# An encoder trunk on one core: thirteen weight units split ahead by half units, five output-weight units split where they are used, and attention's visits in another order

## The chip, the core and the metric

The kernel runs on one core of one Trainium2 chip. The metric is device time of one execution in microseconds (us). The engines are named as in the profile: PE is TensorE (PEld its weight loads), DVE is VectorE, ACT is ScalarE, POOL is GpSimd, and SP is SyncE, which issues the DMA transfers. "Granted clock" is the share of full speed at which the profile shows TensorE clocked.

## The reference

One inference step of a two-layer encoder for two groups of frames, 1024 of a prompt and 32 of a sample. Layer 0 mixes with an mLSTM, layer 1 with windowed attention (16 query heads, 2 key heads, its own chunk of 64 frames and the two before). Behind each mixer stands an output product and a LayerNorm, then a gated FFN and a LayerNorm. What the change touches of it:

```python
D_MODEL, D_FF, DEPTH = 1024, 2816, 2

def swiglu(x, w_gu, w_down):
    g, u = jnp.split(x @ w_gu, 2, axis=-1)
    return (jax.nn.silu(g) * u) @ w_down

def sink_attention(q, k, v, sinks, bias):
    s = jnp.einsum('bcqhgd,bckhd->bchgqk', q, k).astype(F32) * (HEAD_DIM ** -0.5) + bias
    sk = sinks.astype(F32).reshape(N_KV_HEADS, GROUP)[:, :, None, None]
    mx = jnp.maximum(jnp.max(s, -1, keepdims=True), sk)
    p = jnp.exp(s - mx)
    p = p / (jnp.sum(p, -1, keepdims=True) + jnp.exp(sk - mx))
    return jnp.einsum('bchgqk,bckhd->bcqhgd', p.astype(v.dtype), v)

def swa_prompt(x, k, v, w_q, sinks, w_out, slopes):
    q = (x @ w_q).reshape(B, nc, CHUNK, N_KV_HEADS, GROUP, HEAD_DIM)
    ...
    o = sink_attention(q, kw, vw, sinks, bias)
    return o.reshape(B, T, D_ATT) @ w_out

def trunk(...):
    for layer in range(DEPTH):
        ...
        x = layer_norm(DEEPNORM_ALPHA * x + mix, ln_g[layer, 0], ln_b[layer, 0])
        x = layer_norm(DEEPNORM_ALPHA * x + swiglu(x, w_gu[layer], w_down[layer]), ln_g[layer, 1], ln_b[layer, 1])
```

All of it is in fp32.

## The kernel before, in words

**Numbers.** Every fp32 operand of a dense product is split into a high part (a cast to fp32r) and a low part (the operand less its high part, also fp32r). A k step of `gemm` is then three matmuls: high by high (L433), high by low (L434), low by high (L435). So each weight and each activation needs a cast and a subtraction ahead of its use. Activations live as `act` (fp32) and `sx` (both parts), `split_act` makes the second from the first (cast L463, subtraction L464). The 1056 columns of activations go in three groups `GRP` of 384, 384 and 288 for projections, and in four quarters of 264 for output products.

**Order.** One host-side program emits all instructions; each engine runs its own in the order of emission. The dense products are emitted one behind the other, and each k step calls `tick(us)` with its written length. Other work stands in generator tasks, launched on a `Weave`: a task emits some instructions and yields the us until it wants to go on, so that written pauses, not a scheduler, set where its instructions stand among the dense ones. `drain` runs a task ahead without pauses until a condition holds.

**Weights.** A weight unit is 128 rows by 1024 columns, split as two half units (u,0) and (u,1) of 128x512. The class `Weights` loads units into a ring of four raw tiles `wr` and makes, in one fixed order, the split tiles `wh`, `wl` (L250 to L260): the cast on ScalarE (L258), or on GpSimd (L256) for halves listed in `on_gpsimd`, which is empty before; the subtraction on VectorE for halves in `on_vector` and on GpSimd else (both L260). `home` tiles (`oh`) hold the halves that stay resident. Units listed in `ready` are not split there: their parts are read from a tile in DRAM, `halves`.

**The split ahead.** `split_before` (L1312 to L1330) fills `halves` during layer 0's FFN. It is launched at the FFN's seventh factor product, stands beside the FFN's up product, and covers 18 units: 2 of `wkv`, 8 of `wqb` (query weights), 8 of `wout_b` (attention's output weights). It has one raw tile `wraw` of 128x1024 and one tile `whi` of 128x512. For a unit it loads `wraw`, yields 9.0, and for each half casts into `whi` (L1322), yields 1.5, subtracts in place (L1324), yields 1.8, stores both parts (L1327) and yields 4.5 or 2.0.

**The down product.** Behind the up product, `down` multiplies by the FFN's second weight through seven factor products of half size. Its `put` adds each PSUM tile (A or B) to `act` on VectorE: L1587 for the first sum of a cell, L1589 for the others.

**Attention.** Sixteen heads go in eight pairs, j. A visit (jp, g) is the pairs j = 2jp and 2jp+1 in column group g: `q_group` projects the queries (24 matmuls for each j), and six items of attention follow, three blocks of 128 frames for each j. An item passes six stages in a pipeline: `scores` (matmuls L1879 or L1885 into `psS`, then the bias and a row maximum on VectorE), `soft` (exponent on ScalarE), `scale` (L1910 on VectorE, L1913 or L1917 on GpSimd), `turn` (transposes L1938 into T, cast L1942, subtraction L1943), `values` (L1967 into O), `place` (L1981 on ScalarE, L1985 on VectorE, adding into `act`). `scores` and `turn` yield `GAP_A` = 0.46 us an item, `values` twice that for every second item. The visits go in the order `JG`:

```python
JG = [(jp, 0) for jp in range(4)] + [(jp, g) for jp in range(4) for g in (1, 2)]
```

**The early output tiles.** After a visit (jp, 2) with jp below `EARLY` = 3, `before(0)` sees to it that all of attention's group 0 is placed and its activations are split, and one tile of the output product's first quarter is emitted (`out_tile`, L1265). The rest of the output product, `mixer_out` (L1272), follows after the last visit, with the LayerNorm beside it. `mixed_parts` (L1232) is the task that splits attention's result: 24 casts on ScalarE and 24 subtractions on GpSimd. Unit lists: `U_QB` are query weights, `U_OUT_B[0]` the output weights for the first three quarters, `U_OUT_B[1]` the same weights a second time for the last.

## Time and profile before

| what | value |
|---|---|
| runs | 3: 2203.27, 2203.59, 2203.68 us |
| median | 2203.59 us |
| profiled execution | 2202.94 us |
| its span (first to last recorded instruction) | 2201.2 us |
| mean granted clock of TensorE | 0.995 |

The profiled execution stands beside the runs, 0.65 us below their median; all durations quoted below are of it. In its rows, "A <- B" at a tile reads "A is written from B", x is a count, and a row of the timeline is: start in us from the span's start, duration, engine, line, operation, tiles, shapes, and in brackets how long the engine had been idle just ahead and who ended that. The row of a window gives its limits and length, then busy us and instructions of PE, PEld, DVE, ACT and POOL, the granted clock, the mean share of the 16 DMA engines and GB/s.

### The profile page before, as it was taken

How to read it: one execution, taken by the hardware profiler on the slowest of the kernel's cores; microseconds unless marked ns; L12 is line 12 of the kernel's file. 1: busy time of each engine (PE TensorE's matmuls, PEld its weight loads, DVE VectorE, ACT ScalarE, POOL GpSimd, SP SyncE). 2: the span in 40 equal slices, each digit the busy share in tenths (PEclk: the TensorE clock that was granted, in tenths of full speed). 3: DMA queues.
4: the chain of work that ended last, by engine and by line, in shares of the span. 5: the costliest groups of instructions: out<-in, count | busy, mean ns of one | idle time of the engine just before them, and what ended most of it. 6: DMA issues, size and time to landing. Idle time of an engine off the chain costs nothing.

```text
span 2201.2 us, 44080 instructions
## 1 busy us (share of the span) xinstructions
PE 2166.9 (98%) x16982; PEld 2142.1 (97%) x16982; DVE 1469.2 (67%) x2822; ACT 995.0 (45%) x2243; POOL 917.1 (42%) x928
## 2 busy tenths in 40 slices
PE   9999999999999999989999999999999999999997
PEld 9999999999999999989999999999999999999997
DVE  4465676788777776556657776788666566466657
ACT  4443455465444444321235676656444444431125
POOL 2544310004666665444432443500665555554441
PEclk9999999999999999999999999999999999999999
DMA  5221212212665666797617542611344433497712
GB/s 171 77 63 57 58 40 87 89 39 86 216 220 204 226 207 208 267 329 263 190 52 234 163 126 85 223 49 39 128 147 157 147 138 147 137 350 249 251 53 80
DMA packets 191250, 332.99 MB, mean 151 GB/s; under 512 B 19200, under 2 KB 124728, under 8 KB 191040
## 3 DMA queue, kind: packets, MB, share of 16 engines
q1 hardware_dynamic: 186688, 325.84, 44.3%
q10 hardware_dynamic: 4352, 4.33, 0.6%
q8 instruction: 134, 2.20, 0.4%
q14 instruction: 76, 0.62, 0.1%
HBM read 226.47 MB, written 101.82 MB: 149 GB/s over the span
## 4 chain that ended last, share of the span: by engine, by line
PE 87%; DVE 5%; DMA 4%; ACT 3%; issue 1%; SPq 0%; POOL 0%; ACTq 0%; DVEq 0%; POOLq 0%
PE d L433 11%; PE d L435 10%; PE d L434 10%; PE A L433 9%; PE A L435 9%; PE A L434 9%; PE B L433 7%; PE B L434 7%; PE B L435 7%; PE O L1967 1%; DMA sx<-hs_t 1%; PE psS L1879 1%; PE T L1938 1%; ACT act L536 1%; PE T L986 1%
## 5 line engine op out<-in xcount | busy, mean ns | idle before, releaser
L260 POOL TENSOR_TENSOR wl_s<-wr,wh_s 128x512 fp32r<-128x512 f32 x224 | 309.9, 1394 | 250.9 <-ACT wh_s L258 194.8
L433 PE MATMUL d<-sx,wh 128*128 128x264 f32 (+2 forms) x1040 | 331.9, 319 | 0.0
L260 POOL TENSOR_TENSOR wl_a<-wr,wh_a 128x512 fp32r<-128x512 f32 x112 | 158.5, 1419 | 395.3 <-ACT wh_a L258 390.2
L435 PE MATMUL d<-sx,wl 128*128 128x264 f32 (+2 forms) x1040 | 316.5, 304 | 2.4 <-POOL wl L260 2.4
L434 PE MATMUL d<-sx,wh 128*128 128x264 f32 (+2 forms) x1040 | 316.0, 304 | 0.5 <-POOL sx L464 0.5
L433 PE MATMUL A<-sx,wh_s 128*128 128x264 f32 x896 | 255.7, 285 | 4.5 <-DVE act L1587 4.5
L434 PE MATMUL A<-sx,wh_s 128*128 128x264 f32 x896 | 255.2, 285 | 0.0
L435 PE MATMUL A<-sx,wl_s 128*128 128x264 f32 x896 | 255.0, 285 | 0.0
L258 ACT CAST wh_s<-wr 128x512 fp32r<-128x512 f32 x224 | 135.5, 617 | 193.5 <-DVE wr L201 99.2
L433 PEld LDWEIGHTS d<-sx,wh 128*128 128x128 f32 x1040 | 196.4, 189 | 3.1 <-ACT wh L258 0.2
L435 PEld LDWEIGHTS d<-sx,wl 128*128 128x128 f32 x1040 | 195.8, 188 | 3.2 <-POOL wl L260 2.9
L434 PEld LDWEIGHTS d<-sx,wh 128*128 128x128 f32 x1040 | 196.6, 189 | 1.8 <-POOL sx L464 0.7
L433 PE MATMUL d<-sx,ex 128*128 128x264 f32 x624 | 180.8, 290 | 0.1
L434 PE MATMUL d<-sx,ex 128*128 128x264 f32 x624 | 177.2, 284 | 0.0
L435 PE MATMUL d<-sx,ex 128*128 128x264 f32 x624 | 176.9, 284 | 0.0
L433 PEld LDWEIGHTS A<-sx,wh_s 128*128 128x128 f32 x896 | 169.6, 189 | 4.7 <-ACT wh_s L258 4.7
L435 PEld LDWEIGHTS A<-sx,wl_s 128*128 128x128 f32 x896 | 169.8, 190 | 0.0
L434 PEld LDWEIGHTS A<-sx,wh_s 128*128 128x128 f32 x896 | 169.6, 189 | 0.0
L1383 POOL TENSOR_TENSOR z<-z 128x528 fp32r<-128x528 f32 x76 | 104.8, 1380 | 116.7 <-ACT z L1382 101.4
L433 PE MATMUL A<-ex,wh_s 128*128 128x264 f32 x448 | 127.5, 285 | 0.0
L434 PE MATMUL A<-ex,wh_s 128*128 128x264 f32 x448 | 127.1, 284 | 0.0
L435 PE MATMUL A<-ex,wl_s 128*128 128x264 f32 x448 | 127.1, 284 | 0.0
(374 smaller groups left out, 7155.4 us busy)
## 6 DMA issues: line engine op xcount, KB each, us to landing
wr<-in_gu SPq DMA_DIRECT2D x92, 512.0 KB, 4.0
hs_x<-z SPq DMA_DIRECT2D x72, 528.0 KB, 3.0
hs_t<-z SPq DMA_DIRECT2D x64, 528.0 KB, 3.2
sx<-hs_x SPq DMA_DIRECT2D x112, 264.0 KB, 5.8
sx<-hs_t SPq DMA_DIRECT2D x64, 264.0 KB, 6.2
ex<-hs_t SPq DMA_DIRECT2D x64, 264.0 KB, 6.1
wr<-in_dn SPq DMA_DIRECT2D x32, 512.0 KB, 6.1
wh<-halves SPq DMA_DIRECT2D x46, 256.0 KB, 2.9
```

What stands on the lines that cost most here:

```text
L258: self.nc.scalar.copy(hi, r)
L260: eng.tensor_sub(lo, r, hi.bitcast(F32))
L433: nc.tensor.matmul(out, ah, bh, start=start and k == 0, stop=False, **kw)
L434: nc.tensor.matmul(out, ah, bl, start=False, stop=False, **kw)
L435: nc.tensor.matmul(out, al, bh, start=False, stop=stop and k == last, **kw)
L536: nc.scalar.activation(z, z, AF.Identity, scale=gk, bias=bk)
L986: nc.tensor.matmul(pc[:, : 2 * (DV + 1)], keys, vt[j][:, c], start=True, stop=True)
L1383: eng.tensor_sub(lo.bitcast(F32R), buf(s), hi)
L1879: nc.tensor.matmul(ps[:rows, at : at + nk], lhs, k[:, k0 : k0 + nk], start=i == 0, stop=i == 1)
L1938: nc.tensor.transpose(pt[:nk, t, :rows], p[:rows, at : at + nk], ident[:rows, :rows])
L1967: nc.tensor.matmul(out, v[:nk], x, start=i == 0, stop=i == len(todo) - 1)
```

## The change

1. *Split ahead.* It covers 13 units (of `wout_b` only the first three), and goes by half units with two raw tiles of 128x512, each next half being loaded two us of written time ahead of the cast of the one at hand. There is still one `whi`. `stored` counts halves.
2. *Late output weights.* The other five `wout_b` units of `U_OUT_B[0]` are loaded raw and split in `_next`: half 0 with its cast on ScalarE and its subtraction on VectorE, half 1 with both on GpSimd. The halves of the first two units of `U_OUT_B[1]` have their subtractions on VectorE in place of GpSimd.
3. *Activation splits of attention's result.* Of 24 subtractions the even k go to VectorE, the odd k stay on GpSimd. Casts of group 0 with even k go to GpSimd.
4. *Visits.* The first four stay, then (0,2), (0,1), (1,2), (1,1), (2,2), (2,1), (3,1), (3,2). An early output tile follows the visits (1,2), (2,2) and (3,2) in place of (0,2), (1,2) and (2,2). The gap is 0.43 us, and 0.45 from the seventh visit on.

```diff
--- before.py
+++ after.py
@@ -46,7 +46,7 @@
 RAW = 4
 SLOTS = 5
 GAP_M = (0.6, 1.666, 1.519, 1.5)
-GAP_A = 0.46
+GAP_A = (0.43, 0.45)
 
 FEED_W = 1.7
 
@@ -232,7 +232,7 @@
         ready = u in self.ready
         self.load_to(u if f in (0, 1) else u + 1)
         if ready:
-            assert self.ready[u] in self.stored
+            assert (self.ready[u], f) in self.stored
             w = self.units[u].shape[-1] // 2
         else:
             r = self._source(u, f)
@@ -371,18 +371,20 @@
         U_QB[0] += [add("wqb", u) for u in range(b, b + 4)]
     for jp in range(QH // 4):
         U_QB[1] += [add("wqb", 2 * jp + i) for i in range(2)]
-        if jp < EARLY:
-            U_OUT_B[0].append(add("wout_b", jp))
+        if 0 < jp <= EARLY:
+            U_OUT_B[0].append(add("wout_b", jp - 1))
     U_OUT_B[0] += [add("wout_b", u) for u in range(EARLY, 8)]
     U_OUT_B[1] += [add("wout_b", u) for u in range(8)]
     add_ffn(1)
     on_vector.update((u, f) for u in U_O + U_OUT_A[0] for f in range(2))
     on_vector.update((u, f) for u in U_OUT_B[1][2:] for f in range(2))
     on_vector.update((u, f) for u in U_Q[:1] for f in range(2))
-    W = Weights(nc, base, units, pairs, on_vector, set())
-    BEFORE = [("wkv", i) for i in range(2)] + [("wqb", i) for i in range(8)] + [("wout_b", i) for i in range(8)]
-    for us in (*U_KV, *U_QB, U_OUT_B[0]):
-        name = "wkv" if len(us) == 2 else "wqb" if us is not U_OUT_B[0] else "wout_b"
+    on_vector.update((u, f) for u in U_OUT_B[1][:2] for f in range(2))
+    on_vector.update((u, 0) for u in U_OUT_B[0][EARLY:])
+    W = Weights(nc, base, units, pairs, on_vector, {(u, 1) for u in U_OUT_B[0][EARLY:]})
+    BEFORE = [("wkv", i) for i in range(2)] + [("wqb", i) for i in range(8)] + [("wout_b", i) for i in range(EARLY)]
+    for us in (*U_KV, *U_QB, U_OUT_B[0][:EARLY]):
+        name = {2: "wkv", 8: "wqb", EARLY: "wout_b"}[len(us)]
         W.ready.update((u, BEFORE.index((name, i))) for i, u in enumerate(us))
     W.early = {up[i] for up in U_UP for i in range(FIRST, FT)}
     wv.feed = W.feed
@@ -459,8 +461,8 @@
         gemm(ps, wcols(u), xcols(g))
         return ps
 
-    def split_act(k, g, low=nc.vector):
-        nc.scalar.copy(sxh[k][g][:], act[k][g][:])
+    def split_act(k, g, low=nc.vector, high=nc.scalar.copy):
+        high(sxh[k][g][:], act[k][g][:])
         low.tensor_sub(sxl[k][g][:], act[k][g][:], sxh[k][g][:].bitcast(F32))
 
 
@@ -1229,7 +1231,7 @@
 
     WHOLE = [(g, range(KT)) for g in range(3)]
 
-    def mixed_parts(src, free, mixed, pauses, low=(nc.vector,), runs=WHOLE):
+    def mixed_parts(src, free, mixed, pauses, high=(nc.scalar.copy,), low=(nc.vector,), runs=WHOLE):
 
 
         for (g, ks), pause in zip(runs, pauses):
@@ -1239,7 +1241,7 @@
             for k in ks:
                 while not mixed(k, g):
                     yield 0.3
-                split_act(k, g, low[k % len(low)])
+                split_act(k, g, low[k % len(low)], nc.scalar.copy if g else high[k % len(high)])
                 if g == 0:
                     nc.sync.dma_start(act[k][g], src[:, k, t0 : t0 + n])
                 elif k % 4 == 3:
@@ -1313,20 +1315,31 @@
 
         ex = ExitStack()
         p = ex.enter_context(pool("before"))
-        raw, hi = new(p, "wraw", [P, D]), new(p, "whi", [P, D // 2], F32R)
-        for i, (name, idx) in enumerate(BEFORE):
-            nc.sync.dma_start(raw[:], A[name][idx])
-            yield 9.0
-            for f in range(2):
-                r = raw[:, f * (D // 2) : (f + 1) * (D // 2)]
-                nc.scalar.copy(hi[:], r)
-                yield 1.5
-                nc.vector.tensor_sub(r.bitcast(F32R), r, hi[:].bitcast(F32))
-                yield 1.8
-                for k, t in enumerate((hi[:].bitcast(F32), r)):
-                    nc.sync.dma_start(W.halves[:, i, f, k, :], t)
-                yield 2.0 if f else 4.5
-            W.stored.add(i)
+        raws = [new(p, f"wraw{i}", [P, D // 2]) for i in range(2)]
+        hi = new(p, "whi", [P, D // 2], F32R)
+        todo = [(i, f) for i in range(len(BEFORE)) for f in range(2)]
+
+        def load(n):
+            i, f = todo[n]
+            name, idx = BEFORE[i]
+            nc.sync.dma_start(raws[n % 2][:], A[name][idx][:, f * (D // 2) : (f + 1) * (D // 2)])
+
+        load(0)
+        yield 4.0
+        for n, (i, f) in enumerate(todo):
+            yield 3.0
+            if n + 1 < len(todo):
+                load(n + 1)
+            yield 2.0
+            r = raws[n % 2][:]
+            nc.scalar.copy(hi[:], r)
+            yield 1.5
+            nc.vector.tensor_sub(r.bitcast(F32R), r, hi[:].bitcast(F32))
+            yield 1.8
+            for k, t in enumerate((hi[:].bitcast(F32), r)):
+                nc.sync.dma_start(W.halves[:, i, f, k, :], t)
+            W.stored.add((i, f))
+            yield 3.7
         ex.close()
 
     def ffn(layer, li, tasks, lx, final):
@@ -1841,13 +1854,19 @@
 
     ast = {"ready": 0, "scored": 0, "placed": 0, "v": 0, "visit": -1}
 
-    JG = [(jp, 0) for jp in range(4)] + [(jp, g) for jp in range(4) for g in (1, 2)]
+    JG = [(jp, 0) for jp in range(4)] + [(jp, g) for jp in range(4) for g in ((2, 1) if jp < 3 else (1, 2))]
     QG = [(2 * jp + i, g) for jp, g in JG for i in range(2)]
 
     def last_item(j, g):
         return 6 * JG.index((j // 2, g)) + 6
 
-    def attention(gap):
+    gaps = [[0.0] * 8, [0.0] * 8]
+
+    def pace(gap):
+        gaps[0][:] = [gap] * 8
+        gaps[1][:] = [0.0, 2 * gap] * 4
+
+    def attention():
         S, pairs_ = {}, {}
 
         def parts(b):
@@ -1989,11 +2008,11 @@
         yield from pipeline(
             [(2 * jp + i, 3 * g + b) for jp, g in JG for b in range(3) for i in range(2)],
             [
-                (scores, lambda j, b: ast["ready"] > QG.index((j, CH[b][3])), 0, (gap,) * 8),
+                (scores, lambda j, b: ast["ready"] > QG.index((j, CH[b][3])), 0, gaps[0]),
                 (soft, always, 0, 0),
                 (scale, always, 0, 0),
-                (turn, always, 2, (gap,) * 8),
-                (values, lambda j, b: ast["v"] > b, 1, (0.0, 2 * gap) * 4),
+                (turn, always, 2, gaps[0]),
+                (values, lambda j, b: ast["v"] > b, 1, gaps[1]),
                 (place, always, 0, 0),
             ],
             (5, 3, 2, 1, 0, 4),
@@ -2004,7 +2023,8 @@
         wv.drain(t)
     wv.launch(v_turn(0, 1.5))
     wv.launch(v_turn(1, 5.0))
-    task = wv.launch(attention(GAP_A))
+    pace(GAP_A[0])
+    task = wv.launch(attention())
     ast["ready"] = 4
     keys_values(2)
     wv.launch(v_turn(2, 2.5))
@@ -2029,12 +2049,14 @@
     for n, (jp, g) in enumerate(JG):
         if n < 2:
             continue
+        if n == 6:
+            pace(GAP_A[1])
         while ast["scored"] < 6 * (n - 1):
             wv.tick(0.25)
         for j in (2 * jp, 2 * jp + 1):
             q_group(j, g)
             wv.launch(q_made())
-            if g != 1:
+            if g != (1 if jp == 3 else 2):
                 W.done(U_QB[g > 0][j])
         if n == 3:
             nparts[0] = 0
@@ -2044,14 +2066,15 @@
                     lambda g: ast["ready"] > QG.index((7, g)),
                     lambda k, g: ast["placed"] >= last_item(k, g),
                     (2.4, 1.5, 1.5, 1.0, 1.0),
-                    (nc.gpsimd,),
+                    (nc.gpsimd.tensor_copy, nc.scalar.copy),
+                    (nc.vector, nc.gpsimd),
                     [WHOLE[0], *((g, ks) for ks in (range(6), range(6, KT)) for g in (1, 2))],
                 )
             )
-        if g == 2 and jp < EARLY:
+        if g == 2 and jp:
             before(0)
-            out_tile(U_OUT_B[0][jp], jp, QUARTERS[0][0])
-            W.done(U_OUT_B[0][jp])
+            out_tile(U_OUT_B[0][jp - 1], jp - 1, QUARTERS[0][0])
+            W.done(U_OUT_B[0][jp - 1])
 
     def finish():
         wv.drain(task)
```

Where instructions stand now, at three places.

VectorE at the begin of layer 0's down product, before: L1587 and L1589 are the down product's sums into `act`, L197 to L201 prepare factor weights, L1324 is the subtraction of the split ahead.

```order
L1589 TENSOR_TENSOR act<-act,B_11508 128x2x264 x2
L1589 TENSOR_TENSOR act<-act,B_11525 128x2x264 x2
L197 TENSOR_TENSOR wr_11171<-wr_11171,wr_11173 128x512
L1324 TENSOR_TENSOR wraw_6663<-wraw_6663,whi_6664 128x512
L1587 SCALAR_TENSOR_TENSOR act<-act,A_11316 128x2x264
L1587 SCALAR_TENSOR_TENSOR act<-act,A_11335 128x2x264
L200 TENSOR_TENSOR wr_11173<-wr_11173 128x512
L201 TENSOR_TENSOR wr_11173<-wr_11173,wr_11171 128x512
```

The same place of VectorE's order after the change, where L1600 and L1602 are the lines of the same sums:

```order
L1602 TENSOR_TENSOR act<-act,B_11486 128x2x264 x2
L1602 TENSOR_TENSOR act<-act,B_11503 128x2x264 x2
L197 TENSOR_TENSOR wr_11158<-wr_11158,wr_11160 128x512
L1600 SCALAR_TENSOR_TENSOR act<-act,A_11299 128x2x264
L1600 SCALAR_TENSOR_TENSOR act<-act,A_11318 128x2x264
L200 TENSOR_TENSOR wr_11160<-wr_11160 128x512
L201 TENSOR_TENSOR wr_11160<-wr_11160,wr_11158 128x512
```

The split's subtraction is gone from between the sums; the last one (L1337 in the new numbering) now stands 35 rows ahead of the first sum L1600 in that order.

TensorE ahead of the first early output tile, before: O and T are attention's PSUM tiles, d the dense products'. The rows are the end of a run of 27 rows of attention with no dense product between them, up to the first three matmuls of the output tile (264 columns).

```order
L1967 MATMUL O_15643<-hi_15557,VZ_14495 128x256
L1967 MATMUL O_15643<-lo_15558,VZ_14495 128x256
L1967 MATMUL O_15643<-hi_15557,VZ_14496 128x256
L1967 MATMUL O_15643<-lo_15558,VZ_14496 128x256
L1967 MATMUL O_15643<-hi_15557,VR 128x256
L1967 MATMUL O_15643<-lo_15558,VR 128x256
L1938 MATMUL T_15656<-ident,s_15480 128x128 x3
L433 MATMUL d_15671<-sx,wh_0_15227 128x264
L434 MATMUL d_15671<-sx,wh_0_15227 128x264
L435 MATMUL d_15671<-sx,wl_0_15228 128x264
```

The start of the first early output tile after the change (L435 to L437 are the three matmuls of a k step, L1986 the values, L1898 the scores):

```order
L1986 MATMUL O_15772<-hi_15667,VR 128x256
L1986 MATMUL O_15772<-lo_15668,VR 128x256
L435 MATMUL d_15706<-sx,wh_1_15610 128x288
L436 MATMUL d_15706<-sx,wh_1_15610 128x288
L437 MATMUL d_15706<-sx,wl_1_15611 128x288
L435 MATMUL d_15793<-sx,wh_0_15663 128x264
L436 MATMUL d_15793<-sx,wh_0_15663 128x264
L437 MATMUL d_15793<-sx,wl_0_15664 128x264
L1898 MATMUL psS_14451<-KH_14065,Q_15601 128x192
L1898 MATMUL psS_14451<-KL_14067,Q_15601 128x192
```

The tile (264 columns) now begins right behind the last k step of a query projection (288 columns), with attention's rows between its own k steps.

GpSimd near the end of attention, before: L464 is the subtraction of activations, L1913 and L1917 scale the attention weights `s`, L260 are the subtractions of weights (`wl`).

```order
L464 TENSOR_TENSOR sx<-act,sx 128x288
L1913 TENSOR_TENSOR s_17312<-s_17312,st_17313 128x384
L260 TENSOR_TENSOR wl_0_17374<-wr_17108,wh_0_17373 128x512
L464 TENSOR_TENSOR sx<-act,sx 128x288
L1917 TENSOR_SCALAR s_17336<-s_17336,st_17337 64x160
L260 TENSOR_TENSOR wl_1_17428<-wr_17108,wh_1_17427 128x512
```

GpSimd there after the change (L466 is the subtraction of activations, L1932 the scaling, L256 the cast):

```order
L1932 TENSOR_TENSOR s_17162<-s_17162,st_17163 128x384
L466 TENSOR_TENSOR sx<-act,sx 128x288
L256 CAST oh_14070<-wr_16716 128x512
L260 TENSOR_TENSOR oh_14071<-wr_16716,oh_14070 128x512
L256 CAST wh_1_17281<-wr_16969 128x512
L260 TENSOR_TENSOR wl_1_17282<-wr_16969,wh_1_17281 128x512
L1932 TENSOR_TENSOR s_17218<-s_17218,st_17219 128x384
L1932 TENSOR_TENSOR s_17247<-s_17247,st_17248 128x384
```

Two casts with their subtractions now stand in a row between scalings, and fewer subtractions of activations.

## The prediction

> **What bounds the kernel now.** I read the page first, then the list of who waited for whom on TensorE (engine, line waited for, total us, times, longest).
>
> ```profile
> span 2201.2 us, 44080 instructions
> PE 2166.9 (98%) x16982; PEld 2142.1 (97%) x16982; DVE 1469.2 (67%) x2822; ACT 995.0 (45%) x2243; POOL 917.1 (42%) x928
> PE A L433 <- DVE act L1587: 6.2, 3, 4.5
> PE B L433 <- DVE act L1589: 3.0, 1, 3.0
> PE O L1967 <- DVE act L1985: 2.8, 2, 2.1
> PE d L435 <- POOL wl L260: 2.4, 2, 1.7
> PE d L434 <- POOL sx L464: 0.5, 1, 0.5
> ```
>
> The reader is to see a TensorE that is busy 98% of 2201.2 us. The change adds and removes no matrix product, so all it can win is idle time of TensorE and what comes with it. The list says where that lies: 9.2 us at L1587 and L1589 (the down product of an FFN adding its result to `act`), 2.8 us in attention (L1967), 2.9 us where weights or activations are split late (L260, L464). So I looked at these places in order of time.
>
> ```profile
> 936.93 0.62 ACT L1322 CAST whi<-wraw 128x512 fp32r<-128x512 f32 x1 [6.36 <-DMA halves<-whi]
> 937.58 0.69 DVE L1324 TENSOR_TENSOR wraw<-wraw,whi 128x512 fp32r<-128x512 f32 x1 [4.33 <-ACT whi L1322]
> 939.90 1.30 DVE L1589 TENSOR_TENSOR act<-act,B 128x528 f32<-128x528 f32 x2
> 940.65 0.39 PE L433 MATMUL B<-sx,wh_b 128*128 128x264 f32 x1 [3.05 <-DVE act L1589]
> ...
> 968.83 0.62 ACT L1322 CAST whi<-wraw 128x512 fp32r<-128x512 f32 x1 [11.18 <-DMA halves<-whi]
> 969.48 0.69 DVE L1324 TENSOR_TENSOR wraw<-wraw,whi 128x512 fp32r<-128x512 f32 x1 [8.12 <-ACT whi L1322]
> 970.09 1.31 DVE L1587 SCALAR_TENSOR_TENSOR act<-act,A 128x528 f32<-128x528 f32 x2
> 970.94 0.56 PE L433 MATMUL A<-sx,wh_s 128*128 128x264 f32 x1 [4.50 <-DVE act L1587]
> ```
>
> This is one chain, twice. ScalarE's cast of a half unit into the single tile `whi` waits until the store of the half before it has left that tile (6.36 and 11.18 us idle). VectorE's subtraction of the same half waits for the cast, and the down product's additions (L1589, L1587) stand behind it in VectorE's queue. Only they free the PSUM tile that TensorE wants next. It stands still for 3.05 and 4.50 us.
>
> **The split ahead: 18 units before, 13 after.** What the two stops cost beyond their idle time shows in the windows (PE busy, PEld, DVE, ACT, POOL, granted clock, DMA share, GB/s):
>
> ```profile
> 530.00:930.00 400.00, 400.00 (x3296) 400.00 (x3295) 282.79 (x291) 185.73 (x333) 246.41 (x173) 1.00 0.62 217
> 930.00:966.00 36.00, 32.43 (x253) 32.04 (x252) 19.78 (x30) 7.87 (x15) 14.95 (x11) 0.95 1.01 354
> 971.00:980.00 9.00, 9.00 (x56) 9.00 (x57) 5.05 (x9) 1.15 (x3) 5.32 (x5) 0.72 1.07 387
> ```
>
> After each stop the clock is down: 36 us at 0.95 lose 36 x 0.05 = 1.8 us, 9 us at 0.72 lose 9 x 0.28 = 2.5 us. With the idle time that makes 3.05 + 4.50 + 1.8 + 2.5 = 11.9 us. A second way to the same number is the other layer. Its down product is the same code on the same shapes, with no split beside it:
>
> ```profile
> L1587 DVE SCALAR_TENSOR_TENSOR act<-act,A x16: 689/698/706, 930.4 to 982.2; 128x528 f32<-128x528 f32 x16
> L1589 DVE TENSOR_TENSOR act<-act,B x64: 689/703/707, 939.9 to 1102.3; 128x528 f32<-128x528 f32 x64
> L1587 DVE SCALAR_TENSOR_TENSOR act<-act,A x16: 695/703/705, 1948.6 to 1989.2; 128x528 f32<-128x528 f32 x16
> L1589 DVE TENSOR_TENSOR act<-act,B x64: 691/703/706, 1953.1 to 2109.4; 128x528 f32<-128x528 f32 x64
> ```
>
> From the first L1587 to the last L1589 start, layer 0 takes 1102.3 - 930.4 = 171.9 us and layer 1 takes 2109.4 - 1948.6 = 160.8 us (these are answers of two windows, one per layer). The difference is **11.1 us**, and I take it, since it holds whatever small waits the stage keeps anyway.
>
> Does the new split end ahead of the down product? Rows of the split before:
>
> ```profile
> L1322 ACT CAST whi<-wraw x36: 602/621/625, 541.7 to 968.8; 128x512 fp32r<-128x512 f32 x36
> L1324 DVE TENSOR_TENSOR wraw<-wraw,whi x36: 679/1168/1809, 543.3 to 969.5; 128x512 fp32r<-128x512 f32 x36
> ```
>
> Thirty-six halves took 968.8 - 541.7 = 427.1 us, 35 steps of 12.2 us, against pauses written as 22.1 for two halves, 11.05 each: real time is 1.10 of written time. The new task writes 12.0 for a half and the same 9.0 ahead of the first, so 25 steps of 13.2 us after 541.7 put its last cast near 872, some 58 us ahead of 930.4. VectorE's order agrees: behind the last subtraction of the split come about 35 rows of the up product. New work in this stage is 26 loads of 256 KB in place of 18 of 512 KB on SP. The up product hides all of it now (400.00 busy us of 400.00) and has 10 halves fewer to carry. The new task writes 3.7 + 3.0 + 2.0 = 8.7 between a store and the next cast into `whi`, where the old one wrote 4.5 inside a unit, so ScalarE's waits for `whi` get fewer there. I book 0 for this stage; were its cover gone, the worst that these rows show is one more stop of 4.5 + 2.5 = 7 us.
>
> **Attention's visits.** Before, the first early output tile follows the q projections of visit 5, and the emitter must first finish all of attention's group 0. TensorE's order shows 27 rows of attention there with no dense product between them. On the chip:
>
> ```profile
> 1284.89 0.85 DVE L1985 TENSOR_TENSOR act<-O,t 64x256 f32<-64x256 f32 x2
> 1285.89 0.36 PE L1967 MATMUL O<-hi,VR 128*128 128x256 f32 x1 [2.05 <-DVE act L1985]
> 1280.00:1290.00 10.00, 7.67 (x47) 6.99 (x46) 8.29 (x35) 8.30 (x28) 4.55 (x6) 0.83 0.36 115
> ```
>
> In these 10 us TensorE is idle for 10 - 7.67 = 2.33 us and its clock is 0.83, which loses up to 10 x 0.17 = 1.7: together **4.0 us**. In the changed order the tile comes a visit later and no such bare run is left; every second or third attention step has a dense step beside it. I take the 4.0 us whole. It could be 0, if the two visits that now come one behind the other bring a wait of the same size, and waits elsewhere in attention (T L1938 and others) could move by 2 us either way.
>
> **Late output weights.** Five units (10 halves) are now loaded raw and split beside attention: five casts on ScalarE with subtractions on VectorE, five casts with subtractions on GpSimd. Two further units move their four subtractions from GpSimd to VectorE, half of the 24 activation subtractions (L464) do so too, and four activation casts go to GpSimd. The prices:
>
> ```profile
> L464 POOL TENSOR_TENSOR sx<-act,sx 128x384 fp32r<-128x384 f32 x16 | 16.6, 1042 | 6.9 <-ACT sx L463 6.8
> L464 POOL TENSOR_TENSOR sx<-act,sx 128x288 fp32r<-128x288 f32 x8 | 7.3, 920 | 1.8 <-ACT sx L463 1.8
> L260 POOL TENSOR_TENSOR wl<-wr,wh 128x512 fp32r<-128x512 f32 x4 | 5.3, 1326 | 0.2 <-ACT wh L258 0.2
> L1816 POOL CAST VZ<-VR 64x128 fp32r<-64x128 f32 x28 | 8.1, 290 | 13.2 <-DVE VR L1754 9.2 <-PE O L1967 3.1
> L906 POOL CAST xs<-sx x2: 393/652/912, 20.0 to 20.9; 128x256 fp32r<-128x256 f32 x2
> L260 DVE TENSOR_TENSOR ex<-wr,ex 128x512 fp32r<-128x512 f32 x12 | 8.9, 772 | 1.4 <-ACT ex L258 1.4
> 1390.00:1417.00 27.00, 26.86 (x216) 25.77 (x216) 17.99 (x65) 20.34 (x63) 19.25 (x23) 1.00 0.63 212
> ```
>
> A GpSimd cast of 512 columns is in no row. It lies between 0.65 us (256 columns) and 1.38 us (290 ns for 128 columns, 652 for 256, carried on in a straight line); I take 1.3, near the upper end, so a cast with its subtraction is 2.6 us. Over the last 30 us of attention GpSimd gains 5 x 2.6 = 13 us and loses four L260 (5.3 us) and eight L464 (four of each size, 7.8 us): nothing on balance. Its longest burst, two pairs in a row, holds 4 x 1.3 = 5.2 us. Behind it stands a scaling whose transpose TensorE reaches after about 13 dense steps of 3 x 0.12 us and 3 us of attention, some 8 us later, so it fits.
>
> VectorE is the engine that fills up. It is busy for 18.0 of 27 us. It gains five L260 and three of the four others in this stretch (8 x 0.68 = 5.5 us) and eight activation subtractions (about 4 us), 9.5 in all, while an early tile of 2.9 us dense work moves in: 27.5 of 29.9 us. At the end the wait at L435 (1.7 us) does not go: the half it waits for, once GpSimd's, now stands on VectorE behind the tile sums of the LayerNorm, and its start there is about the end of its old one. ScalarE gains 5 x 0.61 us on 20.34 and stays below VectorE. I book **+2.0 us** for new waits on VectorE. The bounds are -2.1 (the waits of 1.7 and 0.5 go after all) and +6.
>
> A VectorE subtraction of 128x512 took 0.68 us at least, 1.17 in the middle and 1.81 at most in the L1324 row. [...]
>
> **The sum.** -11.1 - 4.0 + 2.0 = -13.1 us on the profiled execution's 2202.94 (its span of 2201.2 and 1.7 around it), so 2189.8. The median of the runs, 2203.59, lies 0.65 above that execution: 2190.5, said as **2190**.
>
> **Rivals.**
> - *VectorE becomes the bound at attention's end.* For: 27.5 of 29.9 us is nearly full, and 13 added subtractions at 1.17 in place of 0.68 add 6.4 us, so 33.9 in 29.9: 4.0 us of stop, and one fall of the clock of about 1.7. Against: some of the splits can be done ahead of need. It gives 2203.6 - 15.1 + 5.7 = 2194, and up to 2199 if group order brings back the 4.0 us.
> - *The change does not do what it says*: the split still reaches into the down product since SP's queue or DMA holds it up. For: the DMA share is above 1.0 in 930 to 980. Against: 58 us of margin. Only attention's 4.0 us would be left: 2199.6.
> - *Slower*: GpSimd's bursts hold the scalings, the transposes wait, and each stop is like the one at 1285.89 (2.05 us and 1.7 of clock). Six tiles stand in that stretch; six such stops are 22.5 us: 2203.6 - 15.1 + 22.5 = 2211. It decides from (8 - 0.83) / 4 = 1.8 us a piece on (0.83 is the scaling itself), and L260 takes 1.33 there. It is unlikely.
> - *More goes than I book*: all listed waits of attention and the late splits vanish: 2190.5 - 4.1 - 2.0, about 2184.
>
> **How the numbers follow.** Forecast (2186 to 2193) 0.60, VectorE bound 0.24, not what it says 0.08, more goes 0.05, slower 0.03. The range leaves out the slower case, the unfinished split and the last bit of "more goes": 2184 to 2198. A measurement of this kernel can tell about 0.2% (4.4 us) from no change, so faster means below 2199.2: 0.60 + 0.05 + nearly all of 0.24 = 0.88; the same 0.09; slower 0.03.
>
> **What would show it.** In the changed profile the waits of TensorE at L1587 and L1589's successors in layer 0 are gone, and that stage lasts about 161 us; the last cast of the split starts before 900; no window of 10 us around the first early tile has a clock under 1. If VectorE's subtractions in attention take about 1.2 us and TensorE waits for VectorE in its last 30 us, the first rival is right. A stop in 530 to 930, or a layer 0 down stage still near 170 us, would prove the main term wrong.

## The result, and the profile after

The changed kernel took 2192.61 us in the median of five runs, against 2203.27 of the kernel before on the same chip. The ratio is 0.9949, with a 95% interval of 0.9934 to 0.9965. The forecast was 2190, with 2186 to 2193 as the likeliest case's own range and 2184 to 2198 as the whole. One of the five runs took 4278.14 us at a granted clock of 1.00, for a reason that nothing on record shows; the median of the other four is 2192.56. The profiled execution took 2192.83.

First the page and the list of who waited for whom on TensorE (engine, tile, line, then the releasing engine, tile and line; total us, times, longest):

```profile
span 2190.7 us, 44028 instructions
PE 2162.7 (99%) x16982; PEld 2136.5 (98%) x16982; DVE 1455.3 (66%) x2833; ACT 991.9 (45%) x2234; POOL 903.3 (41%) x926
```

```profile
PE A L435 <- DVE act L1600: 2.1, 2, 1.2
PE O L1986 <- DVE act L2004: 1.8, 4, 0.7
PE psS L1898 <- DVE st L1904: 1.1, 3, 0.5
PE T L1957 <- POOL s L1932: 1.0, 1, 1.0
PE d L437 <- DVE wl L260: 0.9, 1, 0.9
PE d L437 <- POOL wl L260: 0.7, 1, 0.7
```

The longest stop is now 1.2 us; it stands in layer 1's down product, and layer 0's keeps one of 1.0 us. Those of 4.5 and 3.0 us at the down product are gone, and so is the one of 2.1 us at attention's values. But the values now wait four times in place of twice (1.8 us in sum in place of 2.8), and a transpose waits for GpSimd (L1932), which it did not before.

Where the time went is read from four marks: the first sum of each layer's down product and the last. The rows are one line's instructions in a window; the two numbers behind the durations are the first and the last start. Before, the last sum of layer 0 went to tile A:

```profile
L1589 DVE TENSOR_TENSOR act<-act,A x48: 696/704/706, 984.2 to 1104.6; 128x528 f32<-128x528 f32 x48
```

After, layer 0 (L1600, L1602) and the first sums of layer 1 (the last row):

```profile
L1600 DVE SCALAR_TENSOR_TENSOR act<-act,A x16: 693/704/705, 931.3 to 971.7; 128x528 f32<-128x528 f32 x16
L1602 DVE TENSOR_TENSOR act<-act,A x48: 693/704/706, 973.7 to 1094.1; 128x528 f32<-128x528 f32 x48
L1600 DVE SCALAR_TENSOR_TENSOR act<-act,A x16: 694/704/706, 1937.9 to 1978.9; 128x528 f32<-128x528 f32 x16
```

| stretch of the profiled execution | before | after |
|---|---|---|
| start to the first sum of layer 0 | 930.4 | 931.3 |
| layer 0's down product, first to last sum | 1104.6 - 930.4 = 174.2 | 1094.1 - 931.3 = 162.8 |
| last sum to the first of layer 1 (attention lies in it) | 1948.6 - 1104.6 = 844.0 | 1937.9 - 1094.1 = 843.8 |
| from there to the end of the span | 2201.2 - 1948.6 = 252.6 | 2190.7 - 1937.9 = 252.8 |

All of the gain lies in the down product. The second stretch, for which the prediction booked 2.0 us, gave 0.2. I call the two "the down stage" and "the stretch" below. (The 171.9 of the prediction, and the 160.5 that answers to it, count to the last sum of tile B, 2.3 us earlier.)

The split ahead, and windows of the stage (PE, PEld, DVE, ACT, POOL busy us, granted clock, DMA share, GB/s):

```profile
L1335 ACT CAST whi<-wraw x26: 602/622/624, 542.7 to 863.8; 128x512 fp32r<-128x512 f32 x26
```

```profile
930.00:966.00 36.00, 35.02 (x290) 34.85 (x289) 23.36 (x35) 10.35 (x19) 20.48 (x15) 1.00 1.08 377
1260.00:1290.00 30.00, 28.44 (x204) 26.67 (x204) 21.82 (x85) 21.17 (x70) 13.72 (x22) 1.00 0.45 137
1380.00:1410.00 30.00, 28.94 (x235) 27.87 (x234) 26.11 (x73) 22.39 (x64) 21.62 (x23) 1.00 0.53 156
```

The last cast stands at 863.8, ahead of the first sum. In 930 to 966 the DMA engines are as full as before (a share of 1.08, 1.01 before), yet the clock is 1.00 (0.95 before). In attention the clock is 1.00 too, but TensorE is idle for 1.56 us in the 30 from 1260 and for 1.06 in the 30 from 1380.

The first of these is a chain that one timeline shows (start, duration, engine, line, tiles, in brackets the idle time just ahead and what ended it):

```profile
1263.11 0.83 POOL L1932 TENSOR_TENSOR s<-s,st 128x384 f32<-128x384 f32 x1 [2.24 <-DVE st L1929]
...
1263.89 0.50 POOL L465 CAST sx<-act 128x384 fp32r<-128x384 f32 x1
...
1264.42 0.56 DVE L466 TENSOR_TENSOR sx<-act,sx 128x384 fp32r<-128x384 f32 x1 [0.94 <-POOL sx L465]
...
1264.90 0.84 DVE L2004 TENSOR_TENSOR act<-O,t 64x256 f32<-64x256 f32 x2
...
1265.89 0.35 PE L1986 MATMUL O<-hi,VR 64*128 64x256 f32 x1 [0.60 <-DVE act L2004]
```

The cast of an activation, moved to GpSimd, stands behind a scaling there. VectorE has its subtraction next in its queue and waits for the cast 0.94 us with nothing to do. Behind that stands the addition that frees the PSUM tile O, and TensorE waits for it. The groups of instructions in 1200 to 1450 show that this is no single case (count, then busy us, mean ns, and idle time ahead with what ended it):

```profile
L466 DVE TENSOR_TENSOR sx<-act,sx 128x384 fp32r<-128x384 f32 x8 | 5.9, 734 | 4.3 <-POOL sx L465 3.3 <-ACT sx L465 1.0
L260 DVE TENSOR_TENSOR wl<-wr,wh 128x512 fp32r<-128x512 f32 x10 | 8.3, 834 | 1.2 <-ACT wh L258 1.1
```

The second is GpSimd's burst of late weight splits:

```profile
1390.59 1.07 POOL L256 CAST oh<-wr 128x512 fp32r<-128x512 f32 x1
1391.74 1.29 POOL L260 TENSOR_TENSOR oh<-wr,oh 128x512 fp32r<-128x512 f32 x1
...
1392.97 0.85 POOL L256 CAST wh<-wr 128x512 fp32r<-128x512 f32 x1
1393.90 1.28 POOL L260 TENSOR_TENSOR wl<-wr,wh 128x512 fp32r<-128x512 f32 x1
...
1395.14 2.06 POOL L1932 TENSOR_TENSOR s<-s,st 128x384 f32<-128x384 f32 x2
...
1396.47 0.55 PE L1957 MATMUL T<-ident,s 128*128 128x128 f32 x3 [0.98 <-POOL s L1932]
```

Four instructions hold GpSimd for 1395.14 - 1390.59 = 4.6 us, a scaling waits behind them, and the transposes wait 0.98 us for the scaling. So TensorE was ready for them at 1395.5, 4.9 us after the burst began.

### The profile page after: what moved, and what is told of

Same layout as the page of the kernel before. It is cut to its first block, busy times and chain, and to the rows that moved or that the text cites. A ratio compares the mean times of both kernels' runs of the same rounds, so it can differ in the third digit from the quotient of the medians.

```text
span 2190.7 us, 44028 instructions
## 1 busy us (share of the span) xinstructions
PE 2162.7 (99%) x16982; PEld 2136.5 (98%) x16982; DVE 1455.3 (66%) x2833; ACT 991.9 (45%) x2234; POOL 903.3 (41%) x926
## 4 chain that ended last, share of the span: by engine, by line
PE 86%; DVE 7%; ACT 3%; issue 1%; DMA 1%; POOL 0%; SPq 0%; DVEq 0%; ACTq 0%; POOLq 0%
PE d L435 10%; PE A L435 10%; PE A L437 10%; PE A L436 10%; PE d L437 10%; PE d L436 10%; PE B L435 7%; PE B L436 7%; PE B L437 7%; PE O L1986 1%; PE psS L1898 1%; PE T L1957 1%; DMA hs_x<-z 1%; ACT act L538 1%; PE T L988 1%
## 5 line engine op out<-in xcount | busy, mean ns | idle before, releaser
L260 POOL TENSOR_TENSOR wl_s<-wr,wh_s 128x512 fp32r<-128x512 f32 x224 | 304.2, 1367 | 241.2 <-ACT wh_s L258 181.4
L435 PE MATMUL d<-sx,wh 128*128 128x264 f32 (+2 forms) x1040 | 331.4, 319 | 0.2
L260 POOL TENSOR_TENSOR wl_a<-wr,wh_a 128x512 fp32r<-128x512 f32 x112 | 155.7, 1392 | 401.9 <-ACT wh_a L258 397.7
L437 PE MATMUL d<-sx,wl 128*128 128x264 f32 (+2 forms) x1040 | 316.2, 304 | 1.7 <-DVE wl L260 0.9
L435 PE MATMUL A<-sx,wh_s 128*128 128x264 f32 x896 | 254.5, 284 | 0.0
L437 PE MATMUL A<-sx,wl_s 128*128 128x264 f32 x896 | 254.0, 284 | 0.0
L435 PEld LDWEIGHTS d<-sx,wh 128*128 128x128 f32 x1040 | 196.0, 188 | 3.6 <-ACT sx L465 0.4
L437 PEld LDWEIGHTS d<-sx,wl 128*128 128x128 f32 x1040 | 195.5, 188 | 2.4 <-DVE wl L260 1.4
L435 PE MATMUL d<-sx,ex 128*128 128x264 f32 x624 | 180.7, 290 | 0.1
L437 PE MATMUL d<-sx,ex 128*128 128x264 f32 x624 | 176.9, 284 | 0.0
L437 PEld LDWEIGHTS A<-sx,wl_s 128*128 128x128 f32 x896 | 168.8, 188 | 0.0
L435 PEld LDWEIGHTS A<-sx,wh_s 128*128 128x128 f32 x896 | 168.4, 188 | 0.2 <-issue 0.2
L435 PE MATMUL A<-ex,wh_s 128*128 128x264 f32 x448 | 127.5, 285 | 0.0
L437 PE MATMUL A<-ex,wl_s 128*128 128x264 f32 x448 | 127.1, 284 | 0.0
```

The source lines that it names most:

```text
L260: eng.tensor_sub(lo, r, hi.bitcast(F32))
L435: nc.tensor.matmul(out, ah, bh, start=start and k == 0, stop=False, **kw)
L437: nc.tensor.matmul(out, al, bh, start=False, stop=stop and k == last, **kw)
```

## The experiments

Each kernel was timed beside the kernel before on the same chip; its stretches are read from its profiled execution by the same four marks. The medians of the kernel before were 2202.6 to 2204.0 on these chips.

| kernel | median us | ratio to before (95%) | down stage | stretch | TensorE idle in it |
|---|---|---|---|---|---|
| before | 2203.27 | 1 | 174.2 | 844.0 | 7.4 |
| changed | 2192.61 | 0.9949 (0.9934 to 0.9965) | 162.8 | 843.8 | 7.6 |
| 13 ahead, late splits; old visits | 2192.59 | 0.9955 (0.9942 to 0.9967) | 163.4 | 844.3 | 9.0 |
| visits and gaps alone | 2198.87 | 0.9983 (0.9974 to 0.9991) | 174.0 | 839.6 | 4.3 |
| new staging, 18 units | 2197.06 | 0.9975 (0.9965 to 0.9986) | 169.0 | 843.7 | 7.4 |
| old staging, 13 units, late splits | 2193.57 | 0.9963 (0.9950 to 0.9975) | 163.3 | 846.0 | 9.1 |
| changed, casts of activations on ScalarE | 2190.65 | 0.9942 (0.9930 to 0.9954) | 163.1 | 842.4 | 6.3 |
| changed, activation splits as before | 2190.16 | 0.9939 (0.9926 to 0.9953) | 163.2 | 842.2 | 5.9 |
| 18 ahead hurried, new visits | 2192.47 | 0.9951 (0.9938 to 0.9963) | 165.4 | 839.8 | 4.5 |
| changed, late casts on ScalarE | 2193.66 | 0.9954 (0.9942 to 0.9967) | 163.2 | 845.1 | 7.9 |
| 18 ahead hurried more, new visits | 2190.47 | 0.9944 (0.9931 to 0.9956) | 163.7 | 839.6 | 4.3 |
| order of visits alone, gap 0.46 | 2196.11 | 0.9970 (0.9958 to 0.9982) | 173.7 | 837.5 | 4.6 |
| 15 ahead, three late, new visits | 2187.84 | 0.9933 (0.9921 to 0.9945) | 163.1 | 840.3 | 4.4 |
| the same with gap 0.46 | 2185.81 | 0.9924 (0.9911 to 0.9938) | 163.0 | 837.5 | 4.2 |

The last column is the length of the stretch less TensorE's busy time in it. Every kernel has the same 6591 matmuls there, so what the idle time does not account for is busy time of the same matmuls. Whether gaps too short to be listed hide in that busy time, the traces do not tell.

The kernels ran on several chips, and the intervals of their ratios overlap among the variants. So differences of 1 to 2 us between variants rest on the stretches, of one profiled execution each. Kernels with the same attention agree there within 0.3 us (839.6, 839.8 and 839.6; 844.0 and 843.7), save where the clock falls at one of them and not at the other; that case is shown below.

### The two halves of the change apart

The first kernel has the first two parts of the change on the kernel before (13 units, half-unit staging, the late splits with their engines), with the old visits and the old activation splits. Seen from the changed kernel:

```diff
-GAP_A = (0.43, 0.45)
+GAP_A = 0.46
...
-    JG = [(jp, 0) for jp in range(4)] + [(jp, g) for jp in range(4) for g in ((2, 1) if jp < 3 else (1, 2))]
+    JG = [(jp, 0) for jp in range(4)] + [(jp, g) for jp in range(4) for g in (1, 2)]
...
-                    (nc.gpsimd.tensor_copy, nc.scalar.copy),
-                    (nc.vector, nc.gpsimd),
+                    (nc.gpsimd,),
```

> The first two parts of the change alone: 13 units split ahead by half units, five split where used, the engines of the late weight splits as in the change; visits, gaps and activation splits as before. My theory: the down product's two stops go whole (11.4 us, as the stage lasts 160.5 us in place of 171.9) and late splits cost 0 to 2 us beside attention, so 2192 to 2194 us. Rival, that the order of visits carries a good part of the gain: 2196 us or more. Rival, that the late splits are what ate the gain booked for the visits: the first output tile's stop of 2 us stays and new waits of 2 to 4 us come on top, 2194 to 2196.

It measured 2192.59, with a down stage of 163.4 and a stretch of 844.3. So the down stage's gain belongs to the split ahead. By these two stretches the late splits cost 0.3 us beside the old visits; the kernel with the old staging below shows that the clock hides more. With that, visits and activation splits together bring nothing: the changed kernel is at 2192.61.

The second has the order of visits, the early tiles and the gaps alone, on the kernel before:

```diff
-GAP_A = 0.46
+GAP_A = (0.43, 0.45)
...
-    JG = [(jp, 0) for jp in range(4)] + [(jp, g) for jp in range(4) for g in (1, 2)]
+    JG = [(jp, 0) for jp in range(4)] + [(jp, g) for jp in range(4) for g in ((2, 1) if jp < 3 else (1, 2))]
...
-        if g == 2 and jp < EARLY:
+        if g == 2 and jp:
```

> The order of visits, the early tiles a visit later and the gaps of 0.43 and 0.45 alone; 18 units split ahead as before, nothing split late, activation splits as before. As the prediction booked it (the stop at the first early tile and its clock, 4.0 us): 2199.3 us. Rival, that what is won there comes back at once as many waits of 0.3 to 1 us in attention, whatever is split late: 2202 to 2204. The down product's two stops stay in both.

It measured 2198.87, and its stretch is 839.6: 4.4 us less than before, against 4.0 booked. Rows of its list of waits:

```profile
PE A L433 <- DVE act L1587: 6.5, 3, 5.0
PE B L433 <- DVE act L1589: 3.1, 1, 3.1
PE O L1973 <- DVE act L1991: 0.2, 1, 0.2
```

Both stops of the down product are still there, and the values wait 0.2 us in place of 2.8. The rival fell: the visits do not give their gain back by themselves. Of the 4.4 us, 3.1 are idle time of TensorE (7.4 to 4.3). So something else in the change takes 843.8 - 839.6 = 4.2 us.

### Place or staging

The changed `split_before` on the kernel before, whose list of 18 units stays:

```diff
-        raw, hi = new(p, "wraw", [P, D]), new(p, "whi", [P, D // 2], F32R)
...
+        raws = [new(p, f"wraw{i}", [P, D // 2]) for i in range(2)]
+        hi = new(p, "whi", [P, D // 2], F32R)
```

> The new staging (half units, two raw tiles) with all 18 units, nothing split late, attention as before. My theory, that the place of the last halves decides and not the staging: 35 steps of 12.84 us after 542 end near 992, six halves stand among the down product's sums in place of three, so the stops stay or grow: 2201 to 2210 us. Rival, that two raw tiles keep the cast from waiting: no stop is left, 2192.

It measured 2197.06 with a down stage of 169.0. My theory missed: six halves now stand among the down product's sums, but there are fewer stops, not more. The rival missed as well, since one stop is left:

```profile
PE A L433 <- ACT wh_b L258: 3.9, 1, 3.9
PE A L433 <- DVE act L1598: 1.4, 2, 1.0
```

The new staging writes 8.7 us between a half's stores and the next cast into `whi` in place of 4.5, and the two old stops go. What remains is another chain: ScalarE's weight cast stands behind the FFN's cast L1393, as in the rows of the hurried split below. So the staging does help where the split reaches into the down product.

The old staging with 13 units, on the kernel before:

```diff
-BEFORE = [("wkv", i) for i in range(2)] + [("wqb", i) for i in range(8)] + [("wout_b", i) for i in range(8)]
+BEFORE = [("wkv", i) for i in range(2)] + [("wqb", i) for i in range(8)] + [("wout_b", i) for i in range(EARLY)]
...
+    on_vector.update((u, 0) for u in U_OUT_B[0][EARLY:])
+    W = Weights(nc, base, units, pairs, on_vector, {(u, 1) for u in U_OUT_B[0][EARLY:]})
```

> The old staging (whole units, one raw tile) with 13 units; the late splits as in the change; visits and activation splits as before. My theory, that only the number of units counts: 25 steps of 12.2 us after 542 end near 847, ahead of the first sum at 930, so the same time as the kernel with the new staging and the late splits, within 1 us: 2192 to 2195. Rival, that the single raw tile or its bursts on DMA cost time of their own: 2196 or more.

It measured 2193.57, 1 us above the kernel with the new staging, as my theory had it, with a down stage of 163.3. With 13 units, the staging plays no part in the down stage.

Its profiled execution was 2.2 us above its own median, and its stretch of 846.0 is 1.7 above that of the kernel with the new staging, though both have the same attention. The traces show why. Both stop at the first early tile for 2.06 us, but the clock stays at 1.00 in the one and falls in the other. First the rows of the kernel with the new staging, then of this one:

```profile
1274.80 0.35 PE L1980 MATMUL O<-hi,VR 128*128 128x256 f32 x1 [2.06 <-DVE act L1998]
1270.00:1280.00 10.00, 7.66 (x62) 7.33 (x63) 8.09 (x38) 8.77 (x30) 5.10 (x6) 1.00 0.26 78
...
1276.18 0.35 PE L1969 MATMUL O<-hi,VR 128*128 128x256 f32 x1 [2.06 <-DVE act L1987]
1275.00:1285.00 10.00, 8.68 (x56) 8.51 (x57) 6.99 (x28) 7.94 (x25) 6.17 (x7) 0.83 0.27 72
```

TensorE is idle for 9.0 and 9.1 us of the two stretches, so the 1.7 us are slower matmuls. The kernel before had the fall as well. The 0.3 us above therefore compares a stretch with the fall with one without it. With the fall in both, the late splits cost 846.0 - 844.0 = 2.0 us beside the old visits, of which 1.7 are idle time (7.4 to 9.1).

### What takes the visits' gain back

The changed kernel with one line less of GpSimd's:

```diff
-                    (nc.gpsimd.tensor_copy, nc.scalar.copy),
+                    (nc.scalar.copy,),
```

> The changed kernel, but the casts of attention's group 0 all on ScalarE again; the subtractions still alternate between VectorE and GpSimd. My theory: VectorE's subtractions of even k wait 0.94 us for a GpSimd cast that stands behind a scaling, and the additions into act behind them hold up TensorE (waits at the values of 1.8 us, four times). With the cast on ScalarE at most 0.5 us of them is left; the stretch between the two down products (843.8 us in the changed kernel) gets 1.5 to 2.5 us shorter: 2190 to 2191 us. Rival, that VectorE is simply too full there, by the added subtractions themselves: four stops at the values stay, 2192 to 2193.

It measured 2190.65, with a stretch of 842.4. In its list the values wait 0.5 us:

```profile
PE O L1986 <- DVE act L2004: 0.5, 2, 0.3
```

VectorE has just as many subtractions here. Only the casts that they wait for are on another engine, so the place in the queue was the cost and not VectorE's load. TensorE's idle time in the stretch falls from 7.6 to 6.3 us.

All activation splits as before (casts on ScalarE, subtractions on GpSimd), the rest as in the change:

```diff
-                    (nc.gpsimd.tensor_copy, nc.scalar.copy),
-                    (nc.vector, nc.gpsimd),
+                    (nc.scalar.copy,),
+                    (nc.gpsimd,),
```

> The changed kernel with all activation splits of attention's result as before (casts on ScalarE, subtractions on GpSimd). By my theory the four stops at the values go as well; GpSimd has 12 more subtractions (some 11 us) in attention's last part, where its two casts in a row already hold a transpose up by 1 us, so that one grows to 1.5 to 3 us: stretch 841 to 843, 2190 to 2192 us. Rival, that GpSimd can't carry the late splits beside the activations: stops at the transposes of 4 us and more in sum, 2194 or more. Rival, that the activation splits play no part: 843.8, 2192.6.

It measured 2190.16, with a stretch of 842.2, the same as above within 0.5 us. The wait of a transpose for GpSimd did not grow with the added subtractions:

```profile
PE T L1957 <- POOL s L1932: 1.0, 1, 1.0
PE O L1986 <- DVE act L2004: 0.5, 2, 0.3
```

The part on the transpose missed. The next kernel takes the five late casts off GpSimd:

```diff
-W = Weights(nc, base, units, pairs, on_vector, {(u, 1) for u in U_OUT_B[0][EARLY:]})
+W = Weights(nc, base, units, pairs, on_vector, set())
```

> The changed kernel, but the casts of the five late second halves on ScalarE in place of GpSimd, subtractions on GpSimd as in the change. My theory: the burst of two casts and two subtractions of 4.6 us on GpSimd is what makes a transpose wait 1.0 us for a scaling; without the casts that wait goes, the stops at the values stay: 0.5 to 1.2 us shorter, 2191.5 to 2192. Rival, that ScalarE is the tighter engine: waits for ScalarE's casts or copies of 1 us and more appear, 2193 or more.

It measured 2193.66 with a stretch of 845.1. The transpose's wait for GpSimd is gone from its list, but the time is not better:

```profile
PE O L1986 <- DVE act L2004: 1.9, 4, 0.7
PE psS L1898 <- DVE st L1904: 1.7, 3, 1.0
```

The wait at `psS` grew by 0.6 us. My expectation missed; the direction is the rival's, though the wait that grew names VectorE and not ScalarE. TensorE's idle time in the stretch is 0.3 us more than in the changed kernel and the busy time of the same matmuls 1.0 us more; the list does not show why, and it stays open. This kernel and the changed one were not timed side by side, and are 1.1 us apart.

### Without late splits

The remaining cost, 842.2 - 839.6 = 2.6 us, should be that of the late splits (with the four subtractions that the change moves to VectorE beside them). So all 18 units are split ahead with the new staging, faster, so as to end ahead of the sums, with the new visits and the old activation splits, and the four subtractions are back on GpSimd; in `split_before`:

```diff
-            yield 3.7
+            yield 1.9
```

> All 18 units split ahead with the new staging, but with 1.9 in place of 3.7 at the end of each half, so that the last half ends ahead of the down product; nothing split late; the new visits and gaps; activation splits as before. My theory, that the two gains are independent and only the late splits and the new activation splits ate the second: down stage 163 us as in the changed kernel, stretch between 839.6 as with the visits alone; 2187 to 2189 us. Rival, that the hurried split stops TensorE within the up product or reaches past it: 2192 or more.

It measured 2192.47. The stretch is 839.8 as my theory had it, but the down stage is 165.4, and the first sum comes at 933.2. The time is the rival's and not mine. The last half was cast at 928.9, and this followed:

```profile
942.50 0.64 ACT L1393 CAST z<-z 128x528 fp32r<-128x528 f32 x1 [7.02 <-DMA hs_x<-z]
...
948.07 0.63 ACT L1393 CAST z<-z 128x528 fp32r<-128x528 f32 x1 [3.89 <-DMA hs_x<-z]
...
948.73 0.71 DVE L1394 TENSOR_TENSOR z<-z 128x528 fp32r<-128x528 f32 x1 [6.97 <-ACT z L1393]
...
949.13 0.62 ACT L258 CAST wh_b<-wr 128x512 fp32r<-128x512 f32 x1
...
949.36 1.31 DVE L1598 SCALAR_TENSOR_TENSOR act<-act,A 128x528 f32<-128x528 f32 x2
...
950.16 0.56 PE L433 MATMUL A<-sx,wh_s 128*128 128x264 f32 x1 [3.35 <-ACT wh_b L258]
```

It is the form of the old stops once more, with another task in it: the FFN's own cast L1393 waits for a store of its own tile to leave, and VectorE's sum and ScalarE's weight cast stand behind it. The list puts TensorE's wait down to the weight cast. The pace was then raised further:

```diff
-            yield 1.9
+            yield 0.9
```

> As the run with the hurried split of all 18 units and the new visits, but with 0.9 in place of 1.9 at the end of each half; nothing split late, activation splits as before. There the last half was cast at 928.9, in a stretch where the DMA queues are full (share over 1), and a cast of the FFN's stage waited 7.0 us for its own store; one stop of 3.3 us came of it. My theory, that the split must end ahead of that stretch: 35 steps of about 10 us end near 893, the stop goes, and both gains stand: down stage 163, stretch between 839.7; 2186 to 2188 us. Rival, that the split's transfers now crowd those of the up product: the stop stays or another comes, 2190 to 2193.

It measured 2190.47, with a down stage of 163.7 and a stretch of 839.6. That stop went, as expected, and two small ones (1.7 us) came inside the up product, as the rival had it; the time is the rival's too, and the first sum comes at 932.4, 2.0 us later than before. The larger:

```profile
633.97 0.62 ACT L1333 CAST whi<-wraw 128x512 fp32r<-128x512 f32 x1 [2.53 <-DMA halves<-whi]
...
635.66 0.39 PE L433 MATMUL A<-sx,wh_s 128*128 128x264 f32 x1 [1.24 <-ACT z L1477]
```

Here the cast into `whi` waits for the store, a copy out of PSUM stands behind it on ScalarE, and TensorE waits 1.24 us for that copy. That is the beginning of the prediction's chain, at a place where the kernel before had no stop; it ends in ScalarE's copy in place of VectorE's sum.

Between the two lies a split of 15 units ahead (1.9 at the end of a half) and three late, with the activation splits of before:

```diff
-    BEFORE = [("wkv", i) for i in range(2)] + [("wqb", i) for i in range(8)] + [("wout_b", i) for i in range(EARLY)]
+    BEFORE = [("wkv", i) for i in range(2)] + [("wqb", i) for i in range(8)] + [("wout_b", i) for i in range(5)]
...
-            yield 3.7
+            yield 1.9
```

> The new visits and gaps, 15 units ahead by the new staging with 1.9 at the end of each half, three units split late with the engines of the change, activation splits as before. The split ahead ends near 860. My theory, that each late unit costs its share: with five of them the stretch is 842.2, with none 839.7, so three give 840.5 to 841.5 and the time is 2188 to 2189.5 us. Rival, that the cost hangs on single bursts and not on their number: 842 or more, or 839.7.

It measured 2187.84, with a stretch of 840.3. That is 1.9 us below five late units (842.2) and 0.7 above none (839.6), where an even share of 2.6 / 5 = 0.5 us a unit would give 1.6 above, so the number of units is not all. Of the 1.9 us, 1.5 are idle time (5.9 to 4.4), and 1.0 of them is the transpose's wait for GpSimd, which is not in this list. That the places of the bursts count is likely from it, but was not tried apart.

### The gap

Lastly the order of visits with the old gap, on the kernel before; `GAP_A` stays 0.46 and `attention(gap)` as it was:

```diff
-    JG = [(jp, 0) for jp in range(4)] + [(jp, g) for jp in range(4) for g in (1, 2)]
+    JG = [(jp, 0) for jp in range(4)] + [(jp, g) for jp in range(4) for g in ((2, 1) if jp < 3 else (1, 2))]
```

> The new order of visits and the early tiles a visit later alone, with the old gap of 0.46; everything else as before. My theory, that the order carries the 4.4 us that the visits gave: stretch between the down products 839 to 841 us, time 2198.5 to 2200. Rival, that the order needs the shorter gap, since attention's items fall behind otherwise and a bare run of attention comes back at some tile: 842 to 845, 2201 to 2204.

It measured 2196.11, and the stretch is 837.5. The order alone gives 6.5 us, and the shorter gap costs 2.1 of them. Both of my cases missed, on the good side. The 2.1 us are no listed waits. The waits at `psS`, 0.9 us with the shorter gap, are not in its list, but one of 1.5 at the values is. The stretch of the kernel with the shorter gap, then of this one:

```profile
1103.85:1943.48 839.63, 835.30 (x6591) 824.82 (x6590) 559.96 (x1160) 441.37 (x1023) 364.58 (x364) 1.00 0.41 137
1103.98:1941.47 837.49, 832.91 (x6591) 824.41 (x6590) 561.00 (x1160) 441.19 (x1023) 365.02 (x364) 1.00 0.40 138
```

TensorE is idle for 4.3 and 4.6 us, and busy with the same 6591 matmuls for 835.3 and 832.9. So with the shorter gap the same matmuls are busy 2.4 us longer; why was not tried. Then the best kernel so far with that gap:

```diff
-GAP_A = (0.43, 0.45)
+GAP_A = (0.46, 0.46)
```

> The kernel with 15 units ahead, three split late, the new visits and the old activation splits, but with the old gap of 0.46 throughout. My theory, that the shorter gap costs some 2 us by itself (stretch 839.6 with it and 837.5 without, where nothing is split late): 838 to 839 in place of 840.3, 2185 to 2187 us. Rival, that with late splits beside it the longer gap brings back a bare run of attention or pushes the late splits into the output product: 840 to 843, 2187.5 or more.

It measured **2185.81**, ratio 0.9924 (0.9911 to 0.9938). It beats the kernel before, and its median is 6.8 us below that of the changed one, though the two were not timed on one chip. My theory held, with a stretch of 837.5 just below it. Rows of its list:

```profile
PE O L1986 <- DVE act L2004: 1.2, 1, 1.2
PE d L437 <- DVE wl L260: 1.2, 1, 1.2
```

They are the longest waits left in attention, one at the values and one for a weight split late. A transpose's of 1.0 us and one of 0.7 for GpSimd's half of a weight stand beside them.

## Why the prediction was right, and where a term was off

- **The split ahead: right.** Booked -11.1, measured 162.8 - 174.2 = -11.4. The end of the split was put near 872, and the last cast stands at 863.8; no stop came in 530 to 930 (400.00 busy us of 400.00). The first kernel shows that this part, with the late splits that go with it, makes the whole of the result. That the split ends ahead of the sums is enough: 13 units with the old staging give 163.3, and 18 units, hurried more, 163.7. The new staging alone removes the two stops as well, though six halves stand among the sums, but leaves one of another task (169.0). The chain through the one tile `whi` was argued from the trace of before; the split hurried more shows its beginning at a second place, made by pace alone. A second `whi` was not tried.
- **Visits: right in kind, and only as one part of two.** Booked -4.0 for the bare run of attention, measured -4.4 with the gaps of the change, and no 10 us of attention has a clock under 1.00 now. The prediction priced no gap; the runs show -6.5 for the order and +2.1 for the shorter gap, so that 4.4 lies so near to 4.0 is in part luck. Its 1.7 us for the clock were no sure gain either: the first kernel has the same stop without the fall.
- **Late splits: mis-sized.** The term of the sum that failed is "+2.0 us for new waits on VectorE". It measured 843.8 - 839.6 = +4.2, within the bounds of -2.1 and +6 that it was given. Of it 1.4 us (842.4 against 843.8) come from four casts of activations put on GpSimd, ahead of VectorE's subtractions; with these subtractions back on GpSimd as well it is 1.6. The prediction added up how long GpSimd and VectorE would be busy and did not ask behind what the cast stands and who waits for it. The other 2.6 come with the late splits and the four moved subtractions: 1.6 are idle time of TensorE, 1.0 of it the wait behind GpSimd's burst, and 0.9 busy time of the same matmuls, for a reason that was not tried.
- **"So it fits": wrong.** The burst of two pairs was put at 5.2 us and measured 4.6; the room of some 8 us for the scaling behind it was 4.9, and the transpose waited 0.98. The slower rival's mechanism exists, once and not six times.
- **VectorE as the bound: as full as booked, but not the bound.** It is busy for 27.3 of the 30 us from 1375 and for 26.1 of those from 1380, where 27.5 of 29.9 were booked. TensorE waits for it 0.4 us there (at `psS`) and 0.9 just behind, for a weight, and not 4.0; the clock stays at 1.00, and the kernel with as many subtractions on VectorE but ScalarE's casts loses most of the waits at the values (1.8 us to 0.5). The ten weight subtractions `wl` on VectorE between 1200 and 1450 us, nine of them new, took 834 ns in the mean: six took 0.66 to 0.69 us, like the one such row of before (0.69), two 0.86 and 0.89, and the two longest, 1.23 and 1.29 us, stand beside GpSimd's burst. The rival was priced with the 1.17 of the L1324 row for all; that the moved ones cost as much was its estimate, and these rows do not show it. Its 13 added subtractions leave out three of those that the prediction counts for VectorE.
- **The sum.** -11.4 for the down stage, -0.2 for the stretch in place of -2.0, +0.9 ahead of the first sum and +0.2 behind: -10.5 us of span, where -13.1 was booked. The 2.6 us between them are +2.2 for the late splits, -0.4 for the visits, -0.3 for the split ahead and +1.1 at both ends, which the prediction did not book. The time alone does not tell the forecast from the rival: 2192.61 is 2.6 above 2190 and 1.4 below the 2194 of VectorE as the bound. The stretches and the lists of waits do.
- **Open:** the late splits cost 2.6 us beside the new visits and, with the fall of the clock in both kernels, 2.0 beside the old; the idle time in it is 1.6 and 1.7. What keeps the same matmuls busy up to 2.4 us longer, with the shorter gap above all, is not shown by any run.
